# The low half of a split weight tile: an adding DMA onto ACT's negated high half, or a subtraction on DVE

## The chip, the cores and the metric

The program runs on one core of a Trainium2 chip. The metric is device time in microseconds of one execution; lower is better. Engines are named as the profile names them: PE (TensorE), ACT (ScalarE), DVE (VectorE), POOL (GpSimd) and SP (SyncE).

## The reference, cut to what matters

Two layers of a backbone run over 512 latent tokens and a prefix of 256 context tokens, at width 1024, in float32. Layer 0 is a bidirectional gated linear recurrence (width 2048), layer 1 a chunkwise retention with four heads. At the end stands an RMSNorm of the 512 tokens.

```python
def trunk_layer(x, ctx, c, c_ctx, mod_w, mod_b, norm_g, mixer, need_ctx_out):
    sh, sc, gt = modulation(c[:, None, :], mod_w, mod_b)
    h = rmsnorm(x, norm_g) * (1.0 + sc) + sh
    ...
    y, yc = mixer(h, hc, need_ctx_out)
    x = x + gt * y

# layer 0: u = h @ w_in; conv; r, i = sigmoid(per-block products); scan in both directions;
#          y = ((lat[0] + lat[1]) * silu(u[..., W:])) @ w_out
# layer 1: q, k, v, gate = h @ w_in; rotary; masked scores; y = (silu(gate) * rms(o)) @ w_out
```

## The kernel before

All large products are made from pairs. A float32 operand is split into a high half in the type float32r and a low half, which is the operand minus the high half; a product then takes three matmuls, high x low, high x high and low x high (`mm3`, lines 75 to 78). Weights are split on the chip, tile by tile.

A weight tile is 128 x 1024 (the gate weights `lru_w_g` 128 x 512). SP loads it into `wraw` (`load`, line 82). `split_w` (lines 85 to 93) writes `whi` with a copy on ACT (line 91) and `wlo` with a subtraction on DVE (line 92). The pool `wp` has four buffers each of `wraw`, `whi` and `wlo`.

The list `order` (lines 98 to 113) names all 128 tiles in the order in which they are used: 64 of layer 0 (32 of `lru_w_in`, 16 of `lru_w_g`, 16 of `lru_w_out`) and 64 of layer 1 (48 of `ret_w_in`, 16 of `ret_w_out`). `take` hands out the next tile and has `split_to` split up to three tiles further. So a tile is split when the tile four places ahead of it is used up: the copy into `whi` waits for the last matmul on that buffer.

Layer 0 loops over 16 channel tiles (`iteration`, line 417 and on). In one iteration PE makes the input products of later channel tiles (`mm_in`), four gate products for this one, and one or two units of the output product; PSUM has four slots of 128 x 1024 that go round. ACT empties the gate products with a sigmoid into `g` (line 449), makes exponentials, tanh and square roots (lines 464 to 480), and starts the convolution `xl`. DVE does the rest of the convolution, which reads its input out of a PSUM slot (`x_post`, line 261), the scans (lines 485 to 489) and the low halves. Layer 1 loops over four heads (`do_k`, `do_q`, `do_v`, `do_s`, `do_o`, `do_g`, `do_out`).

The program is traced in the order of the source; a planner then sets the order on each engine. It takes the earliest traced instruction that its own model of durations holds ready, so that work of neighbouring iterations is mixed. A few places name an instruction behind which others have to stand (`tc.issue_after`). On the chip each engine runs its instructions strictly in that order. POOL has nothing but an `iota` (line 630).

At the end of layer 0's loop one tile is split with its copy on DVE (`dve=True`), and two are split by another helper (`split_y`).

Of the kernel before, what the change touches and what calls it, by code (L numbers as in the profile page):

```python
# [7 lines left out]
F32 = mybir.dt.float32  # L8
F32R = mybir.dt.float32r
AF = mybir.ActivationFunctionType  # L10
ALU = mybir.AluOpType
# [32 lines left out]
def backbone(ctx: ExitStack, tc: tile.TileContext, xT, vec, trig, lru_mod_sc, lru_mod_gt, lru_w_in, lru_w_g, lru_w_out,  # L44
             ret_mod_w, ret_mod_gt, crow, ret_w_in, ret_w_out, out):
    nc = tc.nc
# [35 lines left out]
        nc.sync.dma_start(out=t, in_=src)  # L82
        return t

    def split_w(raw, n, pool, dve=False):
        hi = pool.tile([P, n], F32R, tag="whi", name="whi")
        lo = pool.tile([P, n], F32R, tag="wlo", name="wlo")
        if dve:
            nc.vector.tensor_copy(out=hi, in_=raw)
        else:  # L90
            nc.scalar.activation(out=hi, in_=raw, func=AF.Copy)  # L91
        nc.vector.tensor_tensor(out=lo, in0=raw, in1=hi.bitcast(F32), op=ALU.subtract)  # L92
        return hi, lo

    EARLY = (15,)
# [2 lines left out]
    order = [(lru_w_in[0, 0], 1024), (lru_w_in[0, 1], 1024), (lru_w_in[1, 0], 1024)]  # L98
# [14 lines left out]
    raws, ready = [], []  # L113
    pos = [0]

    def fetch_to(i):
        while len(raws) <= min(i, len(order) - 1):
            src, n = order[len(raws)]
            raws.append((load(src, n), n))

    def split_to(i, pool=wp, dve=False):
        i = min(i, len(order) - 1)
        fetch_to(i)
        while len(ready) <= i:
            raw, n = raws[len(ready)]
            raws[len(ready)] = None
            ready.append(split_w(raw, n, pool, dve))

    def split_y(i, t, d, dve):
        fetch_to(i)  # L130
# [12 lines left out]
    def take(n=1, ahead=3):  # L143
        i = pos[0]
        pos[0] += n
        split_to(i + ahead)
        got = ready[i:i + n]
        ready[i:i + n] = [None] * n
        return got if n > 1 else got[0]
# [82 lines left out]
    with ExitStack() as l0:  # L232
# [11 lines left out]
        for k in range(0, KD, 2):  # L244
# [3 lines left out]
                             func=AF.Silu)  # L248
# [33 lines left out]
        with tc.tile_pool(name="mp", bufs=4) as mp, tc.tile_pool(name="mp1", bufs=1) as mp1:  # L282
# [60 lines left out]
            def normed(k):  # L343
# [3 lines left out]
                return t  # L347

            split_to(0)
            with tc.issue_after(spread.ins):  # L350
                rows = mod_mm(0)
# [65 lines left out]
        def iteration(c):  # L417
# [54 lines left out]
            if c == CT - 1:  # L472
                with tc.issue_after(ix[1].ins):
                    split_to(pos[0] + 3, dve=True)
                yt = [(yp.tile([P, NT], F32R, tag="yh", name="yh"), yp.tile([P, NT], F32R, tag="yl", name="yl")) for _ in range(3)]
                with tc.issue_after(qs[0].ins):
                    split_y(pos[0] + 4, yt, 0, True)
# [474 lines left out]
```

## Time and profile before

| | |
|---|---|
| time, median of 3 runs | 1084.69 us (1081.68, 1084.69, 1086.03) |
| span of the profiled execution | 1081.5 us; the profile gives no other time for it |
| PE busy | 1060.7 us, 98% of the span |
| DVE busy | 706.9 us, 65% |
| ACT busy | 573.0 us, 53% |
| POOL busy | 1.1 us |
| moved by DMA | 95.56 MB, mean 88 GB/s |

Busy time is the time in which an engine had an instruction running. Matmuls overlap each other, so that one of 0.39 us is followed by the next after 0.23 us. Times of single instructions are in us from the start of the span; what stands in brackets behind an instruction is the idle time of its engine before it and what ended that. An arrow such as `whi<-wraw` reads: written from.

### The profile page before, as it was taken

To read this page: it belongs to the slowest core of one execution; us is meant where nothing else is said; L and a number is where in the kernel's file an instruction comes from. 1 tells how busy PE (TensorE), PEld (TensorE's weight loads), DVE (VectorE), ACT (ScalarE), POOL (GpSimd) and SP (SyncE) were. 2 spreads that over 40 slices of the span, in tenths; PEclk is the share of its full clock that TensorE was granted. 3 is DMA by queue.
4 is the path that set the end of the run, shared out by engine and by line. 5 is a ranking of instruction groups with operands and counts; after the bars stand their busy time and mean duration, and the time that the engine had idled before them with its cause. 6 is when DMAs were issued, how large, how long until landed. Compare 5 with 4: busy or idle time off the path is not lost.

```text
span 1081.5 us, 15148 instructions
## 1 busy us (share of the span) xinstructions
PE 1060.7 (98%) x6284; PEld 911.8 (84%) x6284; DVE 706.9 (65%) x991; ACT 573.0 (53%) x745; POOL 1.1 (0%) x5
## 2 busy tenths in 40 slices
PE   8999999999999999999999999999999999999996
PEld 7787767888888888888889988899888988889886
DVE  4777667886788687878989755462555525544256
ACT  5657768766687468788366343132432324222254
POOL 0000000000000000000000000000000000000000
PEclk9999999999999999999999999999999999999998
DMA  9624653221222121222213512211122112231102
GB/s 358 224 76 160 203 172 102 68 75 62 69 69 62 56 61 47 75 67 78 75 40 118 195 39 78 98 59 39 59 77 79 59 39 61 76 98 41 39 1 78
DMA packets 29045, 95.56 MB, mean 88 GB/s; under 512 B 2992, under 2 KB 6192, under 8 KB 27952
## 3 DMA queue, kind: packets, MB, share of 16 engines
q1 hardware_dynamic: 28976, 94.59, 26.7%
q8 instruction: 49, 0.80, 0.3%
q14 instruction: 20, 0.16, 0.0%
HBM read 92.48 MB, written 2.10 MB: 87 GB/s over the span
## 4 chain that ended last, share of the span: by engine, by line
PE 67%; ACT 6%; DVE 5%; issue 2%; DVEq 0%
PE ps L76 22%; PE ps L77 22%; PE ps L78 22%; ACT g L465 1%; ACT a L464 1%; DVE g L483 1%; ACT q L467 1%; DVE xl L261 1%; ACT L480 1%; ACT L464 1%; ACT g L449 1%; DVE q L489 1%; DVE q L496 1%; DVE q L495 0%; ACT q L480 0%
## 5 line engine op out<-in xcount | busy, mean ns | idle before, releaser
L91 ACT ACTIVATE whi<-wraw 128x1024 fp32r<-128x1024 f32 (+1 forms) x125 | 124.9, 1002 | 217.4 <-PE ps L77 174.6
L92 DVE TENSOR_TENSOR wlo<-wraw,whi 128x1024 fp32r<-128x1024 f32 (+1 forms) x126 | 144.9, 1152 | 96.4 <-ACT whi L91 75.8
L76 PE MATMUL ps<-hll,whi 128*128 128x512 f32 x496 | 197.3, 398 | 0.0
L77 PE MATMUL ps<-hhl,whi 128*128 128x512 f32 x496 | 194.9, 393 | 0.0
L78 PE MATMUL ps<-hhl,wlo 128*128 128x512 f32 x496 | 193.4, 390 | 0.0
L76 PE MATMUL ps<-yl,whi 128*128 128x512 f32 (+1 forms) x416 | 143.7, 345 | 3.4 <-DVE yl L498 1.6
L77 PE MATMUL ps<-yh,whi 128*128 128x512 f32 (+1 forms) x416 | 142.6, 343 | 0.0
L78 PE MATMUL ps<-yh,wlo 128*128 128x512 f32 (+1 forms) x416 | 142.4, 342 | 0.0
L78 PEld LDWEIGHTS ps<-hhl,wlo 128*128 128x128 f32 x496 | 93.3, 188 | 21.8 <-issue 0.8
L76 PEld LDWEIGHTS ps<-hll,whi 128*128 128x128 f32 x496 | 93.7, 189 | 10.6 <-issue 1.0
L77 PEld LDWEIGHTS ps<-hhl,whi 128*128 128x128 f32 x496 | 93.7, 189 | 10.2 <-issue 1.0
L76 PE MATMUL ps<-hlc,whi 128*128 128x256 f32 x320 | 91.1, 285 | 1.2 <-DVE hlc L226 1.2
L76 PEld LDWEIGHTS ps<-yl,whi 128*128 128x128 f32 x416 | 78.4, 188 | 16.0 <-ACT g L449 2.9
L78 PE MATMUL ps<-hhc,wlo 128*128 128x256 f32 x320 | 90.6, 283 | 0.2 <-DVE wlo L92 0.2
L77 PE MATMUL ps<-hhc,whi 128*128 128x256 f32 x320 | 90.3, 282 | 0.0
L78 PEld LDWEIGHTS ps<-yh,wlo 128*128 128x128 f32 x416 | 78.3, 188 | 10.1
L77 PEld LDWEIGHTS ps<-yh,whi 128*128 128x128 f32 x416 | 78.3, 188 | 9.6
L76 PEld LDWEIGHTS ps<-hlc,whi 128*128 128x128 f32 x320 | 60.3, 189 | 18.4 <-issue 4.1
L77 PE MATMUL ps<-whi,hhl 128*128 128x256 f32 x256 | 72.5, 283 | 0.0
L76 PE MATMUL ps<-wlo,hhl 128*128 128x256 f32 x256 | 72.5, 283 | 0.0
L78 PE MATMUL ps<-whi,hll 128*128 128x256 f32 x256 | 72.4, 283 | 0.0
L77 PEld LDWEIGHTS ps<-hhc,whi 128*128 128x128 f32 x320 | 60.4, 189 | 9.7
(204 smaller groups left out, 2055.7 us busy)
## 6 DMA issues: line engine op xcount, KB each, us to landing
wraw<-in_ret_w_in_dram SPq DMA_DIRECT2D x48, 512.0 KB, 3.5
wraw<-in_lru_w_in_dram SPq DMA_DIRECT2D x32, 512.0 KB, 3.6
mraw<-in_lru_mod_sc_dram SPq DMA_DIRECT2D x8, 1024.0 KB, 9.1
wraw<-in_ret_mod_w_dram SPq DMA_DIRECT2D x16, 512.0 KB, 4.6
wraw<-in_lru_w_out_dram SPq DMA_DIRECT2D x16, 512.0 KB, 3.5
wraw<-in_ret_w_out_dram SPq DMA_DIRECT2D x16, 512.0 KB, 3.6
wraw<-in_lru_w_g_dram SPq DMA_DIRECT2D x16, 256.0 KB, 2.6
wraw<-in_lru_mod_gt_dram SPq DMA_DIRECT2D x8, 512.0 KB, 4.2
```

The source lines that it names most:

```text
L76: nc.tensor.matmul(ps, lhsT=lhs[0], rhs=rhs[1], start=first, stop=False)
L77: nc.tensor.matmul(ps, lhsT=lhs[0], rhs=rhs[0], start=False, stop=False)
L78: return nc.tensor.matmul(ps, lhsT=lhs[1], rhs=rhs[0], start=False, stop=last)
L91: nc.scalar.activation(out=hi, in_=raw, func=AF.Copy)
L92: nc.vector.tensor_tensor(out=lo, in0=raw, in1=hi.bitcast(F32), op=ALU.subtract)
L261: nc.vector.scalar_tensor_tensor(out=t[:, o0:o1], in0=u[:, o0 + sh:o1 + sh], scalar=cw[j], in1=t[:, o0:o1], op0=ALU.mult, op1=ALU.add)
L449: nc.scalar.activation(out=t, in_=ps[:, 256:1024], func=AF.Sigmoid, bias=vt[:, boff:boff + 1])
L464: nc.scalar.activation(out=a, in_=r, func=AF.Exp, scale=sneg[:, d * CT + c:d * CT + c + 1])
L465: nc.scalar.activation(out=r, in_=r, func=AF.Tanh, scale=spos[:, d * CT + c:d * CT + c + 1])
L467: nc.scalar.activation(out=q, in_=a, func=AF.Square)
L480: nc.scalar.activation(out=q, in_=q, func=AF.Sqrt)
L483: nc.vector.tensor_tensor(out=i, in0=i, in1=q, op=ALU.mult)
```

## The change

For tiles at the places 6 to 123 of `order` that are not split with `dve=True`, `split_w` gets the tile's source in HBM. ACT then writes the negated high half into `wlo`, and POOL issues a DMA that reads the raw tile from HBM and adds it onto `wlo`. The raw tile is still loaded by SP, since ACT's first copy reads it. The first six tiles and the last four, the one split with `dve=True` and the two of `split_y` stay as they were.

```diff
-    def split_w(raw, n, pool, dve=False):
+    def split_w(raw, n, pool, dve=False, src=None):
         hi = pool.tile([P, n], F32R, tag="whi", name="whi")
         lo = pool.tile([P, n], F32R, tag="wlo", name="wlo")
         if dve:
             nc.vector.tensor_copy(out=hi, in_=raw)
         else:
             nc.scalar.activation(out=hi, in_=raw, func=AF.Copy)
-        nc.vector.tensor_tensor(out=lo, in0=raw, in1=hi.bitcast(F32), op=ALU.subtract)
+        if src is None:
+            nc.vector.tensor_tensor(out=lo, in0=raw, in1=hi.bitcast(F32), op=ALU.subtract)
+        else:
+            nc.scalar.activation(out=lo, in_=hi.bitcast(F32), func=AF.Copy, scale=-1.0)
+            nc.gpsimd.dma_start(out=lo, in_=src, accum_op=ALU.add)
         return hi, lo
...
         while len(ready) <= i:
-            raw, n = raws[len(ready)]
-            raws[len(ready)] = None
-            ready.append(split_w(raw, n, pool, dve))
+            j, (raw, n) = len(ready), raws[len(ready)]
+            raws[j] = None
+            ready.append(split_w(raw, n, pool, dve, order[j][0] if 6 <= j < len(order) - 4 and not dve else None))
```

## Rows read from the trace of the kernel before

**Rows 1.** The page: busy time and instructions by engine, then 40 slices.
```profile
PE 1060.7 (98%) x6284; PEld 911.8 (84%) x6284; DVE 706.9 (65%) x991; ACT 573.0 (53%) x745; POOL 1.1 (0%) x5
...
PEclk9999999999999999999999999999999999999998
```

**Rows 2.** Stages: length, busy PE, PEld, DVE, ACT, POOL, clock, DMA share, GB/s.
```profile
60.00:530.00 470.00, 462.66 (x2590) 384.71 (x2589) 364.49 (x452) 333.21 (x390) 0.88 (x1) 1.00 0.28 88
530.00:1042.00 512.00, 512.00 (x2923) 450.15 (x2922) 282.87 (x398) 186.64 (x252) 0.00 (x0) 1.00 0.22 71
```

**Rows 3.** Waits of PE, whole span: waiter, releaser, us, times, longest.
```profile
PE ps L76 <- DVE xl L261: 2.1, 3, 0.8
...
PE ps L76 <- DVE yl L498: 1.6, 2, 1.3
PE ps L76 <- ACT g L449: 1.6, 2, 1.4
...
PE ps L76 <- DVE sil L274: 1.3, 2, 0.9
...
PE ps L78 <- DVE wlo L92: 0.2, 1, 0.2
```

**Rows 4.** Groups of split_w by form: count, busy us, mean ns, idle before, releasers.
```profile
L92 DVE TENSOR_TENSOR wlo<-wraw,whi 128x1024 fp32r<-128x1024 f32 x110 | 134.1, 1220 | 88.3 <-ACT whi L91 67.7 <-PE ps L753 20.0
L91 ACT ACTIVATE whi<-wraw 128x1024 fp32r<-128x1024 f32 x109 | 115.1, 1056 | 196.6 <-PE ps L77 153.9 <-PE ps L78 26.4 <-issue 9.6
...
L92 DVE TENSOR_TENSOR wlo<-wraw,whi 128x512 fp32r<-128x512 f32 x16 | 11.0, 687 | 8.1 <-ACT whi L91 8.0
...
L91 ACT ACTIVATE whi<-wraw 128x512 fp32r<-128x512 f32 x16 | 10.0, 628 | 20.8 <-PE ps L77 20.7
```

**Rows 5.** Timeline of ACT in one iteration of layer 0: start, length.
```profile
304.06 1.06 ACT L91 ACTIVATE whi<-wraw 128x1024 fp32r<-128x1024 f32 x1 [1.64 <-PE ps L77]
305.34 1.95 ACT L449 ACTIVATE g<-ps,vt 128x768 f32<-128x768 f32 x2 [0.22 <-PE ps L78]
...
319.43 1.05 ACT L91 ACTIVATE whi<-wraw 128x1024 fp32r<-128x1024 f32 x1
320.38 0.92 ACT L465 ACTIVATE g<-g,spos 128x768 f32<-128x768 f32 x1
```

**Rows 6.** Timeline of PE's weight loads (PEld) and matmuls, the same iteration.
```profile
306.30 0.19 PEld L76 LDWEIGHTS ps<-yl,whi 128*128 128x128 f32 x1 [0.39 <-ACT g L449]
...
308.55 0.39 PE L76 MATMUL ps<-xlo,whi 128*128 128x256 f32 x1 [0.81 <-DVE xl L261]
```

**Rows 7.** Line 449 from 90 to 500 us: who waited, us, times.
```profile
  PEld ps L76: 6.5, 9
```

**Rows 8.** DMA: the queue's packets and share; issues by source, median us to landing.
```profile
q1 hardware_dynamic: 28976, 94.59, 26.7%
...
wraw<-in_ret_w_in_dram SPq DMA_DIRECT2D x48, 512.0 KB, 3.5
...
mraw<-in_lru_mod_sc_dram SPq DMA_DIRECT2D x8, 1024.0 KB, 9.1
```

**Rows 9.** Timeline of PE and ACT: first uses of three tiles, two high halves.
```profile
326.42 0.28 PE L76 MATMUL ps<-hlc,whi 128*128 128x256 f32 x1
...
533.73 1.06 ACT L91 ACTIVATE whi<-wraw 128x1024 fp32r<-128x1024 f32 x1 [0.74 <-PE ps L77]
...
544.81 0.39 PE L76 MATMUL ps<-hll,whi 128*128 128x512 f32 x1
...
822.68 1.06 ACT L91 ACTIVATE whi<-wraw 128x1024 fp32r<-128x1024 f32 x1 [4.49 <-PE ps L77]
...
835.07 0.28 PE L76 MATMUL ps<-wlo,hhc 128*128 128x256 f32 x1
```

**Rows 10.** Timeline of DVE: start of a gapless run, first instruction behind it.
```profile
298.38 1.83 DVE L483 TENSOR_TENSOR g<-g,q 128x768 f32<-128x768 f32 x2 [1.20 <-ACT q L480]
...
317.17 0.96 DVE L268 TENSOR_TENSOR xlo<-xl,xh 128x768 fp32r<-128x768 f32 x1 [2.02 <-ACT xh L267]
```

## Prediction

> **What bounds the kernel now.** I read the page's first two parts, then the table by stage, then what TensorE waits for, and last the order of instructions on each engine inside one pass of the first layer. The page shows PE busy 98% of the span, nearly all of it at the full clock, and DVE (65%) ahead of ACT (53%) [rows 1]. Those averages hide two stages. From 60 to 530 us, the loop over 16 channel tiles of the first layer, PE is busy 462.7 of 470 us, DVE 364.5 and ACT 333.2; from 530 to 1042 us, the second layer, PE is busy the whole 512.0 us, DVE 282.9 and ACT 186.6 [rows 2]. So the second layer can't get faster by anything done off PE, and in the loop 7.3 us are to be had at most. Who ends PE's few waits is listed next: DVE three times over (xl 2.1, yl 1.6, sil 1.3 us, 5.0 in all) and ACT's `g` of line 449 (1.6 us); the split's DVE half, wlo, ended 0.2 us in one wait [rows 3]. What the change takes off DVE was nearly never what PE stood still for.
>
> **The change, part by part.** 128 tiles are ordered; the condition takes places 6 to 123. One of these is split on DVE and two by another helper, so 115 tiles change: 57 in the loop (42 of 1024 columns, 15 of 512) and 58 in the second layer, all of 1024.
>
> *Removed:* a DVE subtraction of 1220 ns, or 687 ns for 512 columns [rows 4]. In the loop 42 x 1.220 + 15 x 0.687 = 61.5 us, so DVE falls from 364.5 to 303.0 us; in the second layer 58 x 1.220 = 70.8 us.
>
> *Added on ACT:* a second copy of the same shape beside the first. The trace has no copy with a scale of -1 here; the nearest row is the first copy itself, 1056 and 628 ns [rows 4], and I take that. In the loop 42 x 1.056 + 15 x 0.628 = 53.8 us, so ACT rises from 333.2 (71% of the stage) to 387.0 us (82%) and passes DVE (64%); in the second layer 61.2 us, to 247.9 of 512 (48%).
>
> *Where the new copy stands.* It is traced right behind the first copy and needs only that one and a buffer that PE frees one matmul later, so I expect it directly behind. ACT works in order. At 304.06 it makes a high half, for which it waited 1.64 us on PE, and at 305.34, after 0.22 us of idling, it starts line 449, the sigmoid that empties a PSUM slot of gate products [rows 5]. PE's weight load at 306.30 is released by that sigmoid, and PE runs behind it with no slack [rows 6]. Over the loop these sigmoids ended nine waits of weight loads (6.5 us, mostly hidden by the running matmul [rows 7]) and two of PE itself (1.6 us [rows 3]). A copy put ahead of such a sigmoid delays it by the copy's pitch, 0.95 us (319.43 to 320.38 [rows 5]), less the idling that it fills, 0.22: 0.73 us, which PE pays. I count it once in each of the 16 iterations: +11.7 us. Bounds: nothing, if every copy falls into ACT's 137 us of idling in this stage (470 less 333.2); +53.8 us, if PE pays every one. I stay near the lower end because only two waits in the trace already reached PE. In the second layer I cost the copies at nothing: ACT there idles 325 us, and its first copies wait on PE 4 us and more (822.68 [rows 9]). Were that cover gone it would be at most 61.2 us.
>
> *Relief by DVE:* half of the 5.0 us of PE waits that DVE ended, so -2.5 us, because DVE's steps on that path themselves wait on ACT sigmoids and exponentials that now come later. Bounds 0 and the stage's 7.3 us.
>
> *Added on POOL and the DMA engines:* 115 adding transfers, which read the raw tile from HBM once more: 100 x 0.524 + 15 x 0.262 = 56.4 MB, since SP still loads the raw tile for the first copy. SP's queue moved 94.59 MB in 26.7% of 16 engines' span [rows 8], so one more plain read is 16%, and twice that if the destination has to be read too: 43 to 59% in all. That hides beside PE, though the window around the layer's modulation loads is fuller. No adding transfer stands in the trace. Lower end of its landing: 3.5 us, the plain load of the same size; upper end: 9.1 us, the 1 MB load; I take 7.0, two of the 3.5 us weight loads, for two operands [rows 8]. PE's first matmul of a tile waits for it, and all of PE's queue stands behind that matmul, so the lead decides. The shortest are at the start of the second layer and at the second v tile of each head: copy ended 534.79, use 544.81, 10.0 us; copy ended 823.74, use 835.07, 11.3 us, the latter in three heads [rows 9]. Less the ACT copy, 9.0 us are left for 7.0: hidden, with 2 us to spare. In the loop the lead is longer: the tile copied at 304.06 to 305.12 [rows 5] is first used at 326.42 [rows 9], 21.3 us later. On POOL the transfer waits for ACT; behind it are only the next transfers and one iota (POOL has 1.1 us of work [rows 1]). SP's queue gains: a raw buffer is free one DVE pass earlier, at most the 1.2 us of that pass, and its loads end hardly a wait now [rows 3]: nothing.
>
> *Sum:* 11.7 - 2.5 = +9.2 us on the profiled 1081.5 us, 1090.7. The median of the runs is 3.2 us above that execution, 1084.7, so 1093.9 us.
>
> **Rivals.** *A, a draw.* The order of instructions is planned, and the planner may put the second copies into gaps of ACT or other matmuls ahead of PE's wait. For it: ACT's 137 us of idling in the loop. Against it: that idling is mostly one order of waiting on PE's buffers, and the copy becomes ready exactly there. Half the cost, 5.8, less the relief: +3.3 us, 1088; from 1081 to 1090.
>
> *B, faster.* DVE's relief decides. PE waits 0.81 us at 308.55 for DVE's conv passes (`xl`), which hold the PSUM slot that it needs [rows 6], and DVE ran without a gap of its own from 298.38 to 315.15 us (317.17 less 2.02) with the scans, the conv passes and three subtractions in it [rows 10]. If ACT's extra copies land in its idling and this run shortens, all 7.3 us go: 1077.4. It decides from the point where fewer than about one copy in eight (7.3 of 53.8 us) delays a PSUM release. Against it: the wait at 308.55 is behind no subtraction, and ACT, not DVE, opens the runs (the idle after it was ended by ACT's `xh` [rows 10]).
>
> *C, the sums land late.* If a transfer needs more than 9.0 us, PE stands still. At 15 us, 6.0 us are short at the first place and 16.1 - 11.3 = 4.8 at each of three heads: +20.4 besides the 9.2, so 1114; at 12 us, 3.0 + 3 x 1.8 = +8.4, so 1102. What could make it late is a start on POOL that has to wait until DVE's gapless run is over, 16.8 us in the loop [rows 10]. The Trainium skill, "SBUF — State Buffer", section "Who interferes with whom", speaks for such a start: GpSimd and DVE share a port pair, and descriptor generation on GpSimd is held off while DVE is in a two-port mode. No run here shows it so far, POOL having no transfers. Against C: DVE's run consists of many single passes under 1.8 us, so a start between two of them costs at most that.
>
> **How the numbers follow.** Forecast 0.58 (own range 1087 to 1104), A 0.22, B 0.10, C 0.10. A measurement of this kernel can tell a difference of about 0.5%, 5.4 us, from none: faster is below 1079.3, slower above 1090.1. Slower: 0.52 of the forecast, all of C and 0.02 of A, 0.64. Faster: B and 0.01 of A, 0.11. The rest, 0.25, is the same. The range goes from 1081, where A begins, to 1109, which takes in C up to about 13 us of landing: less than 2 in 10 is left out.
>
> **What would show it.** Right: ACT at about 82% and DVE at 64% from 60 to 530 us; PE's waits for ACT `g` L449 grown from 1.6 us to some 10; the second layer still 512 us long with no waits for a transfer into wlo; transfers landing in 4 to 9 us. Wrong: waits of PE named after the adding DMA (then C), or PE's busy share in the loop up with shorter DVE waits (then B). The sum fails if the planner changes the order on PE so that the waits fall elsewhere, or if the second copy does not stand behind the first.

## The result, and the profile after

The changed kernel takes 1089.34 us (median of seven runs, 1085.51 to 1090.83) where the kernel before took 1082.53 us beside it (seven runs, 1080.98 to 1086.03). The ratio is 1.0053, 95% interval 1.0042 to 1.0064: slower by 5.7 us, 4.5 to 6.9 (6.8 by the medians), about the least that can be told from no change. That lies in the range and on the side that was forecast, 4.6 us under the forecast time. The reasons are another matter: the term that carried the sum came to nothing, and the loss is at a place that was costed at nothing.

The profiled execution is the fastest of the seven, 1085.51 us, with a span of 1083.7. Its page, against [rows 1]: ACT has 115 instructions more, DVE 115 fewer, and POOL its 115 transfers.

```profile
PE 1058.1 (98%) x6284; PEld 911.8 (84%) x6284; DVE 584.3 (54%) x876; ACT 676.2 (62%) x860; POOL 101.4 (9%) x120
```

The same two stages as in [rows 2], with the same columns:

```profile
60.00:530.00 470.00, 460.70 (x2602) 385.86 (x2602) 309.08 (x398) 378.50 (x448) 50.74 (x58) 1.00 0.60 144
530.00:1042.00 512.00, 508.21 (x2885) 446.14 (x2884) 211.33 (x332) 241.55 (x306) 50.48 (x58) 1.00 0.57 130
```

In the loop ACT is now busy 81% and DVE 66%, close to the 82% and 64% that were worked out. In the second layer, where PE had no gap, 3.8 us are missing from its busy time. The waits of PE over the whole span, against [rows 3], name the place:

```profile
PE ps L76 <- ACT kch L627: 3.8, 1, 3.8
PE ps L76 <- DVE yl L502: 3.4, 1, 3.4
PE ps L76 <- ACT g L453: 2.0, 2, 1.7
PE ps L76 <- DVE xl L265: 2.0, 4, 0.7
...
PE ps L186 <- DMA wraw<-in_ret_mod_w_dram: 1.8, 1, 1.8
```

One new wait, 3.8 us for `kch`, the high half of the context keys. The sigmoids of the gates (line 449 before, 453 now) ended 2.0 us where the forecast had some 10, and no wait is for a transfer into `wlo`. This is how PE stands there; the next fence is PE's timeline (start, length, what is in brackets is the idle time before it):

```profile
584.19 0.28 PE L78 MATMUL ps<-whi,hlc 128*128 128x256 f32 x1
588.26 0.50 PE L76 MATMUL ps<-ql,kch 128*128 128x512 f32 x1 [3.79 <-ACT kch L627]
...
588.83 0.40 PE L76 MATMUL ps<-ql,kch 128*128 128x512 f32 x1
589.07 0.40 PE L77 MATMUL ps<-qh,kch 128*128 128x512 f32 x1
589.30 0.75 PE L78 MATMUL ps<-qh,kcl 128*128 128x512 f32 x1
589.84 0.63 PE L76 MATMUL ps<-ql,kch 128*128 128x512 f32 x1
590.27 0.63 PE L77 MATMUL ps<-qh,kch 128*128 128x512 f32 x1
...
592.82 0.39 PE L76 MATMUL ps<-ql,kh 128*128 128x512 f32 x1
```

PE stands still from 584.5 to 588.3. A microsecond later the matmuls of 512 columns follow each other every 0.43 us instead of every 0.23, until 592.82. A table by stage (columns as in [rows 2]) says why: the granted clock is down, from its upper level of 2.4 GHz to the lower of 1.2 for 3.41 us, and the mean over the four microseconds is 0.67.

```profile
584.00:588.00 4.00, 0.47 (x4) 0.27 (x3) 3.97 (x6) 3.03 (x5) 0.00 (x0) 1.00 1.04 241
588.00:592.00 4.00, 3.74 (x11) 2.82 (x12) 1.90 (x4) 1.96 (x4) 0.86 (x1) 0.67 1.04 358
```

The eight matmuls from 589.30 to 592.82 take 3.52 us where eight at 0.234 take 1.87: 1.65 us more, besides the wait. Why `kch` is late stands in ACT's timeline of the changed kernel:

```profile
582.74 1.05 ACT L657 ACTIVATE tm<-tm 128x1024 f32<-128x1024 f32 x1
583.69 0.57 ACT L627 ACTIVATE vh<-ps 128x512 fp32r<-128x512 f32 x1
585.24 1.06 ACT L91 ACTIVATE whi<-wraw 128x1024 fp32r<-128x1024 f32 x1 [0.97 <-DMA wraw<-in_ret_w_in_dram]
586.20 0.58 ACT L627 ACTIVATE vh<-ps 128x512 fp32r<-128x512 f32 x1
586.67 1.05 ACT L95 ACTIVATE wlo<-whi 128x1024 fp32r<-128x1024 f32 x1
587.62 0.59 ACT L627 ACTIVATE kch<-ps 128x512 fp32r<-128x512 f32 x1
```

and in that of the kernel before at the same place:

```profile
584.18 0.60 ACT L623 ACTIVATE kch<-ps 128x512 fp32r<-128x512 f32 x1
...
591.97 1.06 ACT L91 ACTIVATE whi<-wraw 128x1024 fp32r<-128x1024 f32 x1 [2.79 <-DMA wraw<-in_ret_w_in_dram]
```

Before, `kch` stood ahead of the next tile's copy, and that copy's wait for the raw tile hurt nobody. In the changed kernel the planner's order has `tm` and both copies of that tile ahead of `kch`, so that ACT waits 0.97 us for a load and spends 3 us on work that PE doesn't wait for.

Two stretches of PE's timeline carry the accounts below. The **loop stretch** goes from PE's first matmul `xlo,whi` to the last one ahead of the context keys; the **layer stretch** from there to the first matmul of the final norm (`ones,fs`). Behind the context keys' own matmuls nothing changes: from the 14th matmul behind the first of them to the final norm it is 473.46 to 473.67 us in the runs before, after, 1 to 6, 9 and 12, wherever the copies and the subtractions are done.

| kernel | loop stretch | layer stretch |
|---|---|---|
| before | 509.56 | 476.79 |
| after | 508.56 | 482.57 |

So the change made the loop 1.0 us shorter and the second layer 5.8 us longer. (The spans differ by only 2.2 us because in this execution the clock did not drop at startup, as it did before and in most others. The other six of the changed kernel have a mean granted clock of 0.991 to 0.993 where this one has 0.996; the next run, at 0.992, shows the usual case.) A stretch of 3.41 us at the lower clock can cost up to half of that, 1.7 us, and the loop stretches of runs 1, 2, 3, 5 and 9 hold one near 520 us, while those of the two kernels and of runs 4, 6 and 10 hold none. Differences between these two groups are uncertain by as much.

### The profile page after: what moved, and what is told of

Read it like the earlier page. It is cut to its first block, busy times and chain, and to the rows that moved or that the text cites. A ratio compares the mean times of both kernels' runs of the same rounds, so it can differ in the third digit from the quotient of the medians.

```text
span 1083.7 us, 15399 instructions
## 1 busy us (share of the span) xinstructions
PE 1058.1 (98%) x6284; PEld 911.8 (84%) x6284; DVE 584.3 (54%) x876; ACT 676.2 (62%) x860; POOL 101.4 (9%) x120
## 3 DMA queue, kind: packets, MB, share of 16 engines
q0 software_dynamic: 16560, 56.37, 30.5%
## 4 chain that ended last, share of the span: by engine, by line
PE 82%; ACT 7%; DVE 6%; issue 2%; DMA 2%; SPq 0%; DVEq 0%; ACTq 0%
PE ps L76 27%; PE ps L77 26%; PE ps L78 26%; DVE xl L265 1%; DVE g L487 1%; DMA wraw<-in_lru_w_in_dram 1%; ACT g L469 1%; ACT a L468 1%; ACT q L471 1%; ACT wlo L95 1%; PE ps L329 1%; ACT L484 1%; PE ps L186 1%; DVE q L493 1%; ACT g L453 1%
## 5 line engine op out<-in xcount | busy, mean ns | idle before, releaser
L95 ACT ACTIVATE wlo<-whi 128x1024 fp32r<-128x1024 f32 (+1 forms) x115 | 114.6, 997 | 1.6
L96 POOL DMA_DIRECT2D wlo<-in_ret_w_in_dram x46 | 40.0, 870 | 388.4 <-ACT wlo L95 383.0
```

What stands on the lines that cost most here:

```text
L95: nc.scalar.activation(out=lo, in_=hi.bitcast(F32), func=AF.Copy, scale=-1.0)
L96: nc.gpsimd.dma_start(out=lo, in_=src, accum_op=ALU.add)
```

## The experiments

Three theories. **W**: the loss is one wait for `kch` and the lower clock behind it. **S**, the prediction's: ACT's copies delay the loop's gate sigmoids, and PE pays. **D**: the second read of the raw tiles slows the raw loads. Times of the kernel before beside these runs are 1082.9 to 1083.4 us.

**1. The changed kernel again, unaltered.**

> The changed kernel once more, unaltered, as the yardstick of its neighbours. Theory W (one wait: PE stands 3.8 us for the high half of the context keys at the start of layer 1, and the clock falls behind it): again +5 to +7 us on the kernel before, the wait near 588 us again in the trace with 3.4 us at the half clock behind it. Theory S (the prediction: the copies on ACT delay the sigmoids of the loop): +5 to +7 us, with PE idle in the loop more than 7.3 us. Theory D (the second read of the weights slows the raw loads): +5 to +7 us, with PE's waits for raw loads adding up to most of it.

1089.32 us, ratio 1.0059 (1.0046 to 1.0072). The loop stretch was 508.37, the layer stretch 483.70. The wait for `kch` was longer:

```profile
PE ps L76 <- ACT kch L627: 5.1, 1, 5.1
...
PE ps L76 <- ACT g L453: 2.0, 2, 1.7
```

The clock dropped three times in this execution (startup, behind the `yl` wait near 520, behind the `kch` wait), in the profiled one above only behind the last of these, which goes with the longer time. W stands; the sigmoids' wait is as small as in the first profile.

**2. `kch` first.** The changed kernel with one order given: the tiles that this call of `take` has split are not split ahead of `kch`. PE's order stays that of the changed kernel. (The lines that keep a handle on `kch` are left out.)

```diff
-            do_v(h, 1)
+            w2 = None
+            if h == 0:
+                with tc.issue_after(kch.ins):
+                    w2 = take(2)
+            do_v(h, 1, w2)
```

> The changed kernel with one order of ACT forced: the two tiles that are split for the second half of the values stand behind the copy of the context keys' high half, so that no copy that waits for a raw load stands ahead of it. PE's order is the same to the instruction. Theory W: PE's wait near 588 us falls from 3.8 to under 1 us, no half clock behind it, 5 us less than the changed kernel, so within 2 us of the kernel before. Theory S or D: no change against the changed kernel (within 1.5 us).

1085.03 us, ratio 1.0022 (1.0010 to 1.0035): 4.3 us of run 1's 5.9 (by the medians) are gone with one order. ACT's timeline there, and PE's wait:

```profile
587.66 0.59 ACT L629 ACTIVATE kch<-ps 128x512 fp32r<-128x512 f32 x1
588.48 1.06 ACT L91 ACTIVATE whi<-wraw 128x1024 fp32r<-128x1024 f32 x1 [0.22 <-DMA wraw<-in_ret_w_in_dram]
```

```profile
PE ps L76 <- DVE vl L630: 1.3, 1, 1.3
```

The wait is down to 1.3 us, now for DVE's `vl`, and no low clock follows it. The layer stretch is 478.57: 1.8 us over before, against 5.8. That is W, a little short of its numbers (a wait under 1 us, a time within 2 us of before); the remaining 1.8 us are most of the 2.4 that stay. Here `tm` still stands ahead of `kch` on ACT, and the pass that uses it (`maskc`, 1.23 us) ahead of `vl` on DVE, where before both stood behind; that this makes the 1.3 us was not tried.

**3 and 4. One layer alone.** The condition `6 <= j < len(order) - 4` becomes `6 <= j < 64` (the loop alone), or `66 <= j < len(order) - 4` (the second layer alone).

> Only the 57 tiles of layer 0 (places 6 to 63) are changed, layer 1 splits on DVE as before. Theory S: the whole loss stays, +5 to +9 us. Theory W: -2 to +1.5 us on the kernel before. Theory D: about half, +3 us.

> Only the 58 tiles of layer 1 (places 66 to 123) are changed, layer 0 splits on DVE as before. Theory S: no loss, within 1.5 us of the kernel before. Theory W: the loss is here, +4 to +7 us, if the planner puts the same copies ahead of the context keys' high half. Theory D: about half, +3 us.

The loop alone: 1084.31 us, ratio 1.0008 (0.9996 to 1.0021), no difference; the loop stretch was 509.12 and the layer stretch 476.79, as before. The second layer alone: 1089.7 us, ratio 1.0061 (1.0049 to 1.0074), the whole loss; its layer stretch was 482.41, with the wait for `kch` again 3.8 us. S falls as an account of this kernel: the change of 57 tiles in the loop, copies and relief together, costs nothing that can be measured.

**5. The copies without the transfer.** ACT writes the negated high half, and DVE writes over it with the old subtraction.

```diff
             nc.scalar.activation(out=lo, in_=hi.bitcast(F32), func=AF.Copy, scale=-1.0)
-            nc.gpsimd.dma_start(out=lo, in_=src, accum_op=ALU.add)
+            nc.vector.tensor_tensor(out=lo, in0=raw, in1=hi.bitcast(F32), op=ALU.subtract)
```

> All 115 second copies stay on ACT, but DVE then writes the low half itself by the old subtraction: no adding transfer and no second read of the raw tile, while DVE keeps its work. In this kernel's order on ACT the context keys' high half (kch) stands ahead of the next tile's copies. Theory W (one wait for kch and the half clock behind it is the whole loss): no wait for kch over 1.5 us, PE at the full clock from 560 to 600 us, time within 0.3% of before (up to +3 us). Theory S (ACT's copies themselves cost, by the sigmoids that they delay): +6 to +12 us, as in the changed kernel or more, since DVE's relief is gone too. Theory D (the second read of the raw tiles slows the raw loads): time as before, and the wait for the modulation weights near 138 us at 0.9 us as in before, where the changed kernel had up to 2.4.

1093.34 us, ratio 1.0089 (1.0074 to 1.0104). W's number, within 0.3%, missed. The loop stretch was 516.12, 6.6 us longer. Up to 1.7 us of that is a stretch at the lower clock near 515 us, which the loop of the kernel before doesn't have. So in the loop the copies do cost something, which DVE's relief must have paid back in the changed kernel. But here the subtraction also had to wait for the second copy; run 10 takes that away.

**6. The second layer alone, with `kch` first** (the edits of 2 and 4 together).

> The change in the second layer alone (tile places 66 to 123), with kch's copy forced ahead of the next tile's copies. The second layer alone without that order took +6.6 us. Theory W: the wait for kch (3.8 us) and the half-clock stretch behind it go, and with the loop as in before the time is that of before: within 0.2% (+-2 us). Theory D or any cost of the other 57 copies and adding transfers of the second layer: +2 to +6 us stay.

1084.57 us, ratio 1.0009 (0.9999 to 1.0019), where the same without the order took 1.0061. The layer stretch, 478.55, is that of run 2: 1.8 us over before, with the same wait of 1.3 us for `vl`. Beyond that place the copies and adding transfers of the second layer cost nothing that shows. This settles W for the second layer but for those 1.8 us.

**7. Each gate sigmoid of the loop done twice**, in the kernel before: line 449 stands twice.

> The kernel before with each of the 64 gate sigmoids of the loop done twice, so that each PSUM slot of gate products comes free at least one more ACT pass (0.90 us) later, and ACT has 57 us more to do in the loop (about what the 57 second copies brought). The price of the prediction's step: if a delayed gate sigmoid is paid by PE in each iteration, as the prediction's sum has it (0.73 us, 16 times), this costs at least 16 x 0.90 = +14 us, and up to 64 x 0.90 = +57 us if PE pays each one. Theory W (PE has slack ahead of nearly all of these releases, so ACT's work there is free): under +4 us.

1135.69 us, ratio 1.0485 (1.0464 to 1.0505), +52 us. PE's waits for the sigmoids:

```profile
PE ps L76 <- ACT g L450: 22.8, 9, 8.5
```

The price by the piece can't be read from it: the planner put other work between the two, and ACT loads a function table 107 times instead of 66, at 1.28 us each, so ACT got 110 us more and not 57. But W's number for this run, under +4 us, failed: more work at these sigmoids is not free. What one of them costs is left to run 12.

**8. A landing twice as late.** ACT writes -2 times the high half, the first transfer adds the raw tile, a second one adds the high half.

```diff
-            nc.scalar.activation(out=lo, in_=hi.bitcast(F32), func=AF.Copy, scale=-1.0)
+            nc.scalar.activation(out=lo, in_=hi.bitcast(F32), func=AF.Copy, scale=-2.0)
             nc.gpsimd.dma_start(out=lo, in_=src, accum_op=ALU.add)
+            nc.gpsimd.dma_start(out=lo, in_=hi, accum_op=ALU.add)
```

> The changed kernel with the low half made by two adding transfers in series: ACT writes -2 times the high half, the first transfer adds the raw tile from HBM, the second adds the high half from SBUF. The sum is the same, but it is there some 5 to 6 us later (a landing of 11 to 12 us after ACT's copy in place of 5.5). In the changed kernel the smallest times between a landing and PE's first use were 0.8 us (near 541), 1.4, 2.7, 3.1 and 3.2 us. By the prediction's rival C each microsecond missing is paid by PE once: 4.7 + 4.1 + 3 x 2.7 = some +15 us over the changed kernel (clock not counted), with waits named after the adding transfer near 505 to 545 and at the heads' second v tiles. If the planner's order has more slack there than the traces show, or SP's loads fill in: within 3 us of the changed kernel.

1252.24 us, ratio 1.155 (1.150 to 1.159): +169 us, and neither number was near. The run did not do only what was meant. POOL's timeline:

```profile
760.21 1.16 POOL L96 DMA_DIRECT2D wlo<-in_ret_w_in_dram  x1
769.52 0.87 POOL L97 DMA_DIRECT2D wlo<-whi  x1 [8.15 <-DMA wlo<-in_ret_w_in_dram]
770.14 1.15 POOL L96 DMA_DIRECT2D wlo<-in_ret_w_in_dram  x1
```

The second transfer waits on POOL for the first to land, and the next tile's transfer stands behind it: one tile every 9.9 us where the tiles run densest. It shows what a transfer costs that waits for a transfer on an engine that works in order, not what five microseconds of latency cost. That stays open.

**9 and 10. The two parts of the loop's account by themselves.** Run 9 has the relief alone: no subtraction, no second copy, a plain transfer of the raw tile into `wlo`. Run 10 has the copies beside: the kernel before with a copy into a scratch tile that nobody reads.

```diff
# run 9
-            nc.scalar.activation(out=lo, in_=hi.bitcast(F32), func=AF.Copy, scale=-1.0)
-            nc.gpsimd.dma_start(out=lo, in_=src, accum_op=ALU.add)
+            nc.gpsimd.dma_start(out=lo, in_=src)
# run 10
-            nc.scalar.activation(out=lo, in_=hi.bitcast(F32), func=AF.Copy, scale=-1.0)
-            nc.gpsimd.dma_start(out=lo, in_=src, accum_op=ALU.add)
+            nc.vector.tensor_tensor(out=lo, in0=raw, in1=hi.bitcast(F32), op=ALU.subtract)
+            m = min(n, 1000)
+            nc.scalar.activation(out=junk[:, 0:m], in_=hi.bitcast(F32)[:, 0:m], func=AF.Copy, scale=-1.0)
```

> Only what the change takes away and what it puts on the DMA queue: no subtraction on DVE and no second copy on ACT; the low half is the raw tile itself, brought by a plain transfer of POOL's queue with no adding (the low half is then a wrong number; the instructions on PE are the same). The prediction's relief term is -2.5 us, all of it in the loop; rival B's is -7.3 us. If PE's waits for DVE stand behind steps that were waiting for ACT anyway, nothing: within 1 us of before. From the run with the copies alone, whose loop lost 6.6 us where the changed kernel's lost nothing, I expect the relief in the loop to be worth -3 to -7 us (PE's excess there 27.6 us in the kernel before), so 1077 to 1081. In this order kch stands ahead of the next tile's copies: no wait for it over 1.5 us.

> The kernel before with 115 more ACT copies of the high half, of the same length (1000 of 1024 columns, or 512), written to a scratch tile that nobody reads: DVE's subtraction doesn't wait for them, as it did in the run with the copies alone. Nothing goes off DVE. If the +9.7 us of that run are the price of ACT's time (the prediction's term, +11.7 us): +6 to +12 us again. If they came from DVE's subtraction standing behind the second copy, and with it DVE's later steps: within 2 us of before.

The relief alone: 1078.21 us, ratio 0.9951 (0.9937 to 0.9964), 5.3 us faster by the ratio (4.7 by the medians); the loop stretch is 505.74, 3.8 us shorter, the layer stretch 476.79. The copies alone: 1086.98 us, ratio 1.0039 (1.0027 to 1.0052), 4.1 us slower by the medians; the loop stretch is 513.46, 3.9 us longer. Added up, the loop should gain nothing (+0.1 us); in the changed kernel it was 1.0 us shorter. Run 10 lies between its two theories: a part of run 5's cost was the subtraction behind the copy or the lower clock there, and a part is ACT's time. It isn't paid at the gate sigmoids: in run 10 they ended only 0.4 us of PE's waits, and the longest wait in its loop is 1.5 us for the tile that is split on DVE. Run 9's loop holds a stretch at the lower clock that neither kernel's has, so the relief there lies between 3.8 and 5.5 us; with 5.5 the sum would be -1.6.

**11. The negation on POOL**, to keep the relief and spare ACT.

```diff
-            nc.scalar.activation(out=lo, in_=hi.bitcast(F32), func=AF.Copy, scale=-1.0)
+            nc.gpsimd.tensor_scalar(out=lo, in0=hi.bitcast(F32), scalar1=-1.0, scalar2=None, op0=ALU.mult)
```

> The changed kernel with the negated high half written by POOL (a multiplication by -1) in place of ACT, so that DVE keeps its relief and ACT has nothing more to do. The runs with the parts alone gave -4.7 us for the relief and +4.1 us for the copies on ACT; if POOL's passes are free, the relief stays: some 1078 us (ratio 0.995), which is faster than both kernels. No trace here shows a POOL pass of this size. POOL does the pass and the transfer's issue (0.87 us) one tile after the other, and the landing comes later by as much as its pass takes longer than ACT's 1.0 us; in the changed kernel the smallest time between landing and use was 0.8 us, the next 1.4, 2.7, 3.1 and 3.2. Theory of late landings: with a pass of 3 us or more PE waits for the adding transfer at these places, +5 us or more, half-clock stretches behind the longer waits not counted. Theory of a shared port: DVE's passes get longer (mean of the gates' products and scans up by some per cent) and DVE's waits in the loop come back.

1098.93 us, ratio 1.0144 (1.0118 to 1.0169). POOL's pass and two of DVE's by form (count, busy us, mean ns):

```profile
L95 POOL TENSOR_SCALAR wlo<-whi 128x1024 fp32r<-128x1024 f32 x100 | 289.2, 2892 | 517.6 <-ACT whi L91 517.4
...
L628 DVE TENSOR_TENSOR sl<-sm,sh 128x512 fp32r<-128x512 f32 x24 | 22.1, 922 | 0.3 <-ACT sh L627 0.2
L628 DVE TENSOR_TENSOR vl<-ps,vh 128x512 fp32r<-128x512 f32 x24 | 16.5, 689 | 73.5 <-ACT vh L627 73.5
```

The first of the two passes in the changed kernel, and PE's longest waits in run 11:

```profile
L628 DVE TENSOR_TENSOR sl<-sm,sh 128x512 fp32r<-128x512 f32 x24 | 16.4, 683 | 0.4 <-ACT sh L627 0.3
```

```profile
PE ps L76 <- DVE xl L265: 11.1, 3, 5.5
```

POOL takes 2.89 us for what ACT does in 1.05. `sl`, which has two operands in SBUF, went from 683 ns in the changed kernel to 922; `vl`, with one of its operands in PSUM, stayed at 689 (691). PE's waits for DVE's `xl` in the loop became 11.1 us; late landings cost one wait of 0.4 us. The numbers fit the theory of the shared port and not that of late landings; whether DVE's longer passes alone make the 11.1 us was not separated.

**12. The sigmoids behind the copies.** The loop alone (run 3), and each gate sigmoid not ahead of the last second copy traced before it. No instruction is added.

```diff
+            neg[0] = nc.scalar.activation(out=lo, in_=hi.bitcast(F32), func=AF.Copy, scale=-1.0)
...
+                with tc.issue_after(neg[0].ins) if neg[0] else ExitStack():
                     nc.scalar.activation(out=t, in_=ps[:, 256:1024], func=AF.Sigmoid, bias=vt[:, boff:boff + 1])
```

> The change in the loop alone (which took 0.8 us more than before, its interval touching none), with each gate sigmoid issued no earlier than the last second copy that is traced ahead of it. No instruction is added. Five sigmoids more than there stand directly behind their tile's second copy, among them the first gate's in several iterations, which in the changed kernel stood ahead of the copy (302.48 us before 303.27) and ended waits of PE's weight loads of 0.4 us. If such a sigmoid's delay is paid by PE, as the prediction's step has it (0.73 us each): 5 x 0.73 = +3.7 us over the loop alone, some 1088 us, with longer waits for g. If PE has slack there as well: within 1 us of the loop alone, and the step's price is wrong, not only its count.

1091.31 us, ratio 1.0074 (1.0058 to 1.0090), 7.0 us over the loop alone. In ACT's timeline the sigmoid now stands where the prediction had drawn it:

```profile
312.83 1.06 ACT L97 ACTIVATE wlo<-whi 128x1024 fp32r<-128x1024 f32 x1
313.79 1.68 ACT L456 ACTIVATE g<-ps,vt 128x768 f32<-128x768 f32 x2
```

and PE pays for it; PE's timeline, and then its waits over the span:

```profile
313.48 0.40 PE L78 MATMUL ps<-xh,wlo 128*128 128x512 f32 x1
314.73 0.39 PE L76 MATMUL ps<-yl,whi 128*128 128x256 f32 x1 [0.85 <-ACT g L456]
```

```profile
PE ps L76 <- ACT g L456: 5.7, 6, 1.7
```

Four of the six waits are behind a second copy, 0.49, 1.50, 0.85 and 0.85 us, 3.7 us in all, where in run 3 the same four sigmoids ended 0.3 us: 0.84 us more each. The rest of the 7 us was not taken apart; in this execution the clock also fell behind the wait of 1.50 us. In number the sigmoids directly behind a second copy are 14, as in run 3, and not five more. Five of the 14 are others than there, and four of those are the first gate's of an iteration, the four just named.

## Why the prediction was right in its time and wrong in its reasons

*Durations and loads.* The second copy takes 1054 and 620 ns (1056 and 628 taken from [rows 4]). In the loop ACT rose to 378.5 us (387.0 worked out) and DVE fell to 309.1 (303.0); in the second layer 241.6 (247.9) and 211.3 (212.1). Right, and the differences come from the stage's fixed borders. By form, in the changed kernel, with the columns of [rows 4]:

```profile
L95 ACT ACTIVATE wlo<-whi 128x1024 fp32r<-128x1024 f32 x100 | 105.3, 1054 | 1.6
...
L95 ACT ACTIVATE wlo<-whi 128x512 fp32r<-128x512 f32 x15 | 9.3, 620 | 0.0
```

*"A copy put ahead of such a sigmoid delays it by 0.73 us, which PE pays. I count it once in each of the 16 iterations: +11.7 us."* This step failed, by its count and not by its price. Run 12 has the price: some 0.84 us of waiting where it happens. In the changed kernel it does not happen. Of the 64 gate sigmoids 14 stand directly behind a second copy, which is close to the 16 of the sum, but none of the 14 ended a wait of PE or of its weight loads. Seven other sigmoids did. Three of them stand between their tile's two copies, as the one at 302.48 here, against [rows 5], and four behind `sil` or another gate sigmoid:

```profile
302.48 0.91 ACT L453 ACTIVATE g<-ps,vt 128x768 f32<-128x768 f32 x1
303.27 1.05 ACT L95 ACTIVATE wlo<-whi 128x1024 fp32r<-128x1024 f32 x1
```

The prediction assumed that the new copy would stand directly behind the first wherever that one stands now. The order is planned anew around the new instruction, and the prediction itself named that as the way in which its sum would fail. What was left of the copies' cost in the loop without relief is 3.9 us (run 10).

*Relief by DVE, -2.5 us.* The sign and the place were right, the size too small: -3.8 us or somewhat more in the loop alone, -4.7 us in all (run 9). With the copies' +3.9 it about cancels; the loop of the changed kernel came out 1.0 us shorter, not 9.2 longer.

*"In the second layer I cost the copies at nothing: ACT there idles 325 us."* This step failed, and it is the whole loss: +5.8 us in the layer stretch, of which 3.8 are the wait for `kch` and 1.65 the lower clock behind it (runs 2, 4 and 6). The idling of a stage of 512 us was taken as cover for all of its copies. At the start of the stage there was none: `kch` was made at 584.18, PE wanted it within 3 us, and what stood between them on ACT was a matter of order. That the time came out within 4.6 us is luck: a cost of 11.7 us that did not come, and a loss of 5.8 us at a place that was costed at nothing.

*Landing 7.0 us, hidden with 2 us to spare.* Hidden, with less to spare. From the end of ACT's copy to the landing it was 4.0 to 9.5 us, 5.9 in the median of the 115 transfers; the smallest time left before PE's first use was 0.8 us, at the second of the tiles around 541 us, the first place that the prediction named; the landing there took 7.8 us from its issue. The page's rows, against [rows 8] (median from issue to landing):

```profile
q0 software_dynamic: 16560, 56.37, 30.5%
q1 hardware_dynamic: 28976, 94.59, 26.3%
...
wlo<-in_ret_w_in_dram POOLq DMA_DIRECT2D x46, 512.0 KB, 6.3
wlo<-in_lru_w_in_dram POOLq DMA_DIRECT2D x27, 512.0 KB, 5.3
```

56.8% in all, in the forecast band of 43 to 59%. The one trace of D is the wait for modulation weights in the loop, 0.3 us before and 1.8 after. It doesn't carry the loss: in run 1 it was 0.2 us, and run 1 lost as much. The loads of the raw tiles of 512 KB landed in 3.6 to 3.9 us in the median, against 3.5 to 3.6 before.

*The rivals.* A's time, 1088, came nearest, and its mechanism, a planner that keeps the copies out of PE's way, is what happened in the loop; but the 5.8 us that it left as half of the cost are not in the loop. B's mechanism is real: what is taken off DVE is worth 4.7 us when nothing is put on ACT. C did not occur; POOL's issue began 0.3 to 0.4 us behind ACT's copy each time, also inside DVE's long runs, and took 862 to 1007 ns, so no start was held off. The rule cited there (the Trainium skill, "SBUF — State Buffer", section "Who interferes with whom") concerns a port pair that DVE and GpSimd share, and it hardly spoke for such a start here: by the same section a DVE `tensor_tensor`, which most passes of that run are, has no two-port mode, but with both inputs in SBUF it contends with GpSimd's reads. Run 11, in which POOL computes, agrees with that, by the 922 ns of `sl` and the 689 ns of `vl`.

*What stays open.* Why the planner placed the tile's copies ahead of `kch` was not tried; that the place is the cause was. The wait for `yl` at the end of the loop grew from 1.3 us at most to 3.4 or 3.5 in the changed kernel and in runs 1 to 3 and 12, and to 2.2 in runs 9 and 11, all of them without the subtraction on DVE in the loop; it stayed at 1.1 to 1.4 in runs 4, 5, 6 and 10, which keep it. Why was not tried; its price can't be told from the clock's drops behind it, which come in some executions and not in others. No version here that does the whole computation beats the kernel before.

## What to carry to other kernels

A stage's idle time covers an added instruction only where that instruction is put: look for the few results that the bounding engine takes with no slack, and ask what the new order can put ahead of each, at the borders of the stages first. Where the order is planned, an added instruction moves others, and what it costs may be in their places and not in its own; naming one order (`kch` first) took back 4.3 us of 5.9. And split a sum into runs that hold one term each: relief and cost of about 4 us each hid behind a loop whose time had hardly changed.

## What the runs showed of the hardware

An adding transfer costs more than a plain one of the same bytes. In run 9 the same 56.37 MB went as plain transfers; the page's rows there, beside 30.5% and 5.3 to 6.3 us above:

```profile
q0 software_dynamic: 16560, 56.37, 18.5%
...
wlo<-in_ret_w_in_dram POOLq DMA_DIRECT2D x46, 512.0 KB, 3.9
```

That is 1.7 times the engines' time for adding, for the tiles of 512 KB 1.4 to 1.6 times the landing, and its issue takes POOL 0.87 us against 0.53. The 15 tiles of 256 KB landed alike, in 4.1 us with adding and 4.2 without.

The granted clock fell to 1.2 GHz for 3.41 us (in a few places twice that) behind some of PE's longer waits. Behind the wait for `kch` of 3.8 us it did so in the profiled execution of the changed kernel and of run 4, and behind that of 5.1 us in run 1; behind the 1.3 us of runs 2 and 6 it did not. The length of the wait doesn't decide it alone: behind 1.50 us it fell in run 12 (near 194 us) and not in run 5 (near 190), and behind the 1.7 us that the changed kernel and runs 1 to 3 have near 477 it fell in none. Behind the 3.4 or 3.5 us of `yl` it fell in runs 1, 2, 3 and 12, and not in the changed kernel's profiled execution.
